# A hybrid trunk on one core: up products in passes of 512 and 256 columns, and other start distances between weights and activations

## The chip, the cores and the metric

The kernel runs on one core of a Trainium2 chip. The metric is device time in microseconds (us) of one launch, and less is better. The time before is the median of three runs; one more run was profiled, and its trace is what the sections below quote.

## What is computed

A two-layer trunk over 256 tokens of width 2048, in float32. Layer 0 is differential attention, layer 1 a gated DeltaNet (a chunked linear recurrence); each is followed by the same feed-forward, and each of the four parts is added to the residual `x`. The reference, cut to what matters here:

```python
D_MODEL, SEQ, DEPTH = 2048, 256, 2
D_FF = ((8 * D_MODEL // 3 + 127) // 128) * 128        # 5504 = 43 * 128

def conv_ffn(h, w_up, conv_w, conv_b, w_down):
    u = causal_dwconv(h @ w_up, conv_w) + conv_b       # w_up: 2048 x 11008
    val, gate = jnp.split(u, 2, axis=-1)
    return (jax.nn.silu(gate) * val) @ w_down          # w_down: 5504 x 2048

for i in range(DEPTH):
    h = rms_norm(x, mixer_norm[i])
    x = x + (diff_attention(h, ...) if i % 2 == 0 else gated_deltanet(h, ...))
    x = x + conv_ffn(rms_norm(x, ffn_norm[i]), ffn_w_up[i], ffn_conv_w[i], ffn_conv_b[i], ffn_w_down[i])
```

## The kernel before

Everything is held with the features on the 128 partitions and the 256 tokens along the free axis. A float32 product is made out of float32r matmuls, a shorter format: every weight chunk is cut into a rounded part `whi` (ScalarE, `nc.scalar.copy`, L89) and a remainder `wlo` (VectorE, L90), and every activation tile likewise holds a rounded half and a remainder half side by side, 2 x 256 columns. A product of one 128 x 128 weight tile with one activation tile is then three passes of 256 columns that add up in PSUM: `whi` with the rounded half (L116), `wlo` with the rounded half (L117), `whi` with the remainder half (L118). The text calls these three a **product**. Before each pass TensorE loads the 128 x 128 weights anew (rows PEld in the profile), while the pass before is still streaming.

`dense` makes one **block** of such products: an output of 256 features (two column tiles `c`) by 256 tokens, over `kt` row tiles, in chunks of four row tiles that arrive by one 512 KB DMA each. A block with `kt` = 16 is 32 products or 96 passes. In the order of time the blocks are: 16 for q and k of the attention (`w_qk`), then 4 blocks of `dense_tok` for v (`w_v`), 8 for `w_o`; in the feed-forward 43 up blocks (`w_up`, `kt` = 16, each holds one value tile and one gate tile) and 8 down blocks (`w_down`, `kt` = 43, 86 products each); in the DeltaNet 32 blocks of `w_in`, 8 of `dense_tok` for z and 32 of `w_out` (`kt` = 8) in four groups of heads, among small matmuls of the recurrence; then the second feed-forward. `dense_tok` has the roles turned: activations are the stationary 128 x 128 tile and 512 columns of weights stream past (L137 to L139).

The order of the instructions on an engine is the order in which the code is written, and nothing but semaphores on tiles holds an engine back. PSUM for the blocks is two tiles `ps` of two banks each, taken in turn.

**Distances.** The argument `dist` sets where in its buffer a weight chunk starts. Weight tiles have 128 words of room at their end, and the chunk is written `(place - x) % 128` words behind the tile's start, where `place` is the start of the activations modulo 128 words. So `x` is the distance in four-byte words, modulo 128, from the start of the weights that are being loaded to the start of the activations that stream meanwhile; one number for `whi`, one for `wlo`. Before, q and k, `w_in` and `w_out` take 13, 42, 45 and 12 in turn by head or by group of heads, `w_o`, the gate block, the up blocks of layer 1 from the second on and its down blocks take 51. In layer 0 the up blocks run through a list in which 13, 42 and 45 stand in turn between the values 0, 24, 37, 32, 17, 7 and 48 (so 0, 13, 0, 42, 0, 45, 24, 13, ...), and the down blocks take 13, 0, 13, 42, 0, 42, 45, 51. `dense_tok` has weights and activations at distance 0.

Of the kernel before, what the change touches and what calls it, by code (L numbers as in the profile page):

```python
# [11 lines left out]
ALU = mybir.AluOpType  # L12
# [4 lines left out]
P = 128  # L17
T = 256
# [1 line left out]
KD = D // P  # L20
EPS = 1e-6
CK = 4
BEST = 13, 42, 45
HP, AP, OP = 40, 48, 112
LNEXP = "natural_log_exp_and_others"

# [1 line left out]
class Trunk:  # L28
# [69 lines left out]
    def banks(self):  # L98
        return self.dps.tile([P, 2, 2 * T], F32, tag="ps", name="ps")

    def dense(self, w, kt, acts, place, tiles=2, lead=0, dist=(51, 51)):


        nc = self.nc
        ps = self.banks()
        for k0, nk in self.chunks(kt, CK, lead):
            hi, lo = self.weights(w[:, k0:k0 + nk, :], [(place - x) % P for x in dist])
            steps = [(k, c) for k in range(nk) for c in range(tiles)]
            if k0 + nk == kt:
                steps = [(k, c) for c in range(tiles) for k in range(nk)]  # L110
            for k, c in steps:
                a = acts(k0 + k)
                first, last = k0 + k == 0, k0 + k == kt - 1
                s = slice(c * P, (c + 1) * P)
                o = ps[:, c, :T]
                nc.tensor.matmul(o, hi[:, k, s], a[:, 0, :], start=first, stop=False)  # L116
                nc.tensor.matmul(o, lo[:, k, s], a[:, 0, :], start=False, stop=False)  # L117
                nc.tensor.matmul(o, hi[:, k, s], a[:, 1, :], start=False, stop=last)  # L118
            self.tick()
        return ps  # L120

    def merge(self, ps, u):

        self.nc.vector.tensor_tensor(u, ps[:, :, :T], self.rstd.unsqueeze(1).to_broadcast([P, 2, T]), ALU.mult)  # L124

    def dense_tok(self, w, kt, acts):

        nc = self.nc
        ps = self.banks()
        for k0, nk in self.chunks(kt, CK // 2):  # L130
            hi, lo = self.weights(w[:, k0:k0 + nk, :], (HP, HP))
            for k in range(nk):
                a = acts(k0 + k)
                first, last = k0 + k == 0, k0 + k == kt - 1
                for c in range(2):
                    ah, al = (a[:, i, c * P:(c + 1) * P] for i in range(2))
                    nc.tensor.matmul(ps[:, c, :], ah, hi[:, k, :], start=first, stop=False)  # L137
                    nc.tensor.matmul(ps[:, c, :], ah, lo[:, k, :], start=False, stop=False)  # L138
# [89 lines left out]
    def add_out(self, blk, ps, done):  # L228

        x = self.x[:, 2 * blk:2 * blk + 2, :]  # L230
        self.nc.vector.tensor_tensor(x, ps[:, :, :T], x, ALU.add)
        if done:
            for c in range(2):
                done(2 * blk + c)
            self.add_squares()

    def project(self, w, kt, acts, place, done, final=False, dists=[(51, 51)] * 8):

        n = KD // 2
        for b in range(n):  # L240
            ps = self.dense(w[b], kt, acts, place, dist=dists[b])
            if b < n - final:
                self.add_out(b, ps, done)
                continue
            for c in range(2):
                k = 2 * b + c
                self.nc.vector.tensor_tensor(self.x[:, k, :], ps[:, c, :T], self.x[:, k, :], ALU.add)
                done(k)

    def ffn(self, w_up, w_down, nj, cols_ap, done, final=False):  # L250

        nc = self.nc
        self.spawn(self.norm_stat())
        with self.tc.tile_pool(name="fp", bufs=1) as fp:
            cols = fp.tile([P, 8 * nj + 64], F32, tag="fcols", name="fcols")[:, :8 * nj]
# [3 lines left out]
            if final:  # L259
                ups, downs = [(12, 12)] + [(51, 51)] * (nj - 1), [(51, 51)] * 8  # L260
            else:
                ups = [(x, x) for y in (0, 24, 37, 32, 17, 7, 48) for z in BEST for x in (y, z)] + [(13, 13)]
                downs = [(x, x) for x in (13, 0, 13, 42, 0, 42, 45, 51)]
            rows = self.rows(fp.tile([P, nj * 2 * T + 8], F32R, tag="ac", name="ac"), nj, 0)
            for j in range(nj):
                ps = self.dense(w_up[j], KD, self.h_acts, HP, dist=ups[j])
                c = []
                u = fp.tile([P, 2, T], F32, tag="u", name="u", bufs=2)
                self.merge(ps, u)
# [12 lines left out]

    def attention(self, w_qk, w_v, w_o, nh, dist_ap, ident_ap, qg, kg, lvec, sub, start, done, lambda_init):

        nc, mp = self.nc, self.mp
        with self.tc.tile_pool(name="at", bufs=1) as at:
# [34 lines left out]
            def normed(ps, gain):  # L321
                r = at.tile([P, 2, T], F32, tag="qkr", name="qkr", bufs=3)
                self.merge(ps, r)
                sq = squares(r)
                qn = at.tile([P, 2, T], F32, tag="qkn", name="qkn", bufs=4)

                def go():
                    yield
                    pn = mp()
                    self.total(pn, [sq])  # L330
                    ri = at.tile([P, 2, T], F32, tag="ri", name="ri", bufs=2)
                    self.rsqrt(ri, pn, P)
# [60 lines left out]
            aTs = []  # L393
            for h in range(nh):
                acts, lead = (self.h_acts, 0) if h else (start, 1)
                mine = 2 * ((BEST + (12,))[h % 4],)
                qn, go = normed(self.dense(w_qk[h], KD, acts, HP, lead=lead, dist=mine), qgs)
                self.spawn(go)
                kn, go = normed(self.dense(w_qk[nh + h], KD, self.h_acts, HP, dist=mine), kg)
                aT = at.tile([P, 384], F32, tag=f"aT{h}", name="aT")  # L400
                self.spawn(weigh(h, qn, kn, go, aT))
                aTs.append(aT)
            for h in range(0, nh, 2):
                pv = self.dense_tok(w_v[h // 2], KD, self.h_acts)
# [12 lines left out]
    def gdn(self, w_gate, w_in, w_z, w_out, nb, hb, gate_ap, const_ap, hot_ap, conv_col, ng, done):  # L417
# [12 lines left out]
        with tc.tile_pool(name="gd", bufs=1) as gd:  # L430
# [235 lines left out]

            def out(b, acts):
                for blk in range(KD // 2):
                    ps = self.dense(w_out[b * (KD // 2) + blk], 2 * hb, lambda k: self.await_(acts, k), OP, dist=2 * ((BEST + (12,))[b % 4],))
# [4 lines left out]
            pend = None  # L674
            for b in range(nb):
                heads = range(b * hb, (b + 1) * hb)
                mine = 2 * ((BEST + (12,))[b % 4],)
# [5 lines left out]
                for op, i in plan + [("v", i) for i in range(1, hb)]:  # L683
                    if op == "k":
                        hq = heads[i]
                        c = convs(lin(self.dense(w_in[hq * 2], KD, self.h_acts, HP, dist=mine)), (hq, nq + hq))
                        self.spawn(keys(hq, c, cc, 2 * i, lqs))
                        if i == hb - 1:
                            self.spawn(invert(cc, lqs, inv))
                    elif op == "z":  # L690
                        gr = groups[i]
                        zt = zts[i] = gd.tile([P, 2, gv, P], F32, tag="vz", name="zt", bufs=4)
                        ps = self.dense_tok(w_z[heads[gr[0]] // 2], KD, self.h_acts)
                        for t in range(2):
                            nc.scalar.activation(zt[:, t].rearrange(flat), ps[:, t, :], AF.Silu,
                                                 scale=self.rstdc[:, t:t + 1])
                    else:
                        gi = i // gh
                        gr = groups[gi]
                        if i == gr[0]:  # L700
# [4 lines left out]
                        c = convs(lin(self.dense(w_in[hq * 2 + 1], KD, self.h_acts, HP, dist=mine)),  # L705
                                  (2 * nq + 2 * hq, 2 * nq + 2 * hq + 1))
                        self.spawn(to_tokens(c, vt, 2 * (i - gr[0]), ready))
                if pend:
# [204 lines left out]
```

## Time and profile before

| | us |
|---|---|
| time, median of 3 runs (lowest to highest) | 2715.84 (2714.43 to 2718.64) |
| the profiled run's own time | 2715.1 |
| its span, first to last instruction | 2713.3 |
| TensorE busy | 2699.1 |
| VectorE busy | 1852.9 |
| ScalarE busy | 1453.5 |

The span is what the trace covers, the time has 1.8 us more around it. The ends of matmuls are modelled in such a profile, and matmuls overlap: how fast TensorE goes is read from the distance between the starts of two matmuls, or from the length of a stretch and the number of matmuls in it, and not from its busy share.

### The profile page before, as it was taken

The page shows a single profiled execution, that of the slowest core. Times are in us where ns is not written, and L with a number is a line of the kernel's source. Part 1 is how long each engine was busy: PE and PEld are TensorE (multiplying, and loading weights), DVE is VectorE, ACT ScalarE, POOL GpSimd, SP SyncE. Part 2 cuts the span into 40 slices and gives each one's busy share as a digit, 9 for nine tenths or more (in the row PEclk, how much of TensorE's full clock was granted, in tenths as well). Part 3 has the DMA queues.
Part 4 walks back from the last instruction along what each step waited for, and adds up shares of the span by engine and source line. Part 5 has one row for each costly group of instructions (what it writes and reads, how often), then busy time and mean ns, then how long its engine had stood idle before and what let it go on. Part 6 is the DMA issues. An engine that isn't in the chain of part 4 may idle for free.

```text
span 2713.3 us, 53669 instructions
## 1 busy us (share of the span) xinstructions
PE 2699.1 (99%) x22352; PEld 2628.1 (97%) x22352; DVE 1852.9 (68%) x2719; ACT 1453.5 (54%) x1994; POOL 118.0 (4%) x220
## 2 busy tenths in 40 slices
PE   8999999999999999999999999999999999999999
PEld 8998999999999999999989989999999999999999
DVE  7776566666767554589688688679677777776444
ACT  6555555555555444484574574484465555554333
POOL 0000000000000000012021021021000000000000
PEclk9999999999999999999999999999999999999999
DMA  6555565666666666645355455455456666666665
GB/s 208 168 169 177 157 199 184 188 186 188 191 187 194 178 189 186 184 151 176 123 157 163 140 158 169 140 162 173 128 194 194 195 193 191 196 194 197 204 200 167
DMA packets 135396, 481.62 MB, mean 178 GB/s; under 512 B 15344, under 2 KB 18416, under 8 KB 135152
## 3 DMA queue, kind: packets, MB, share of 16 engines
q1 hardware_dynamic: 134000, 475.57, 57.7%
q8 instruction: 175, 2.87, 0.4%
q10 hardware_dynamic: 1152, 2.61, 0.3%
q14 instruction: 69, 0.57, 0.1%
HBM read 476.03 MB, written 2.10 MB: 176 GB/s over the span
## 4 chain that ended last, share of the span: by engine, by line
PE 99%; ACT 0%; DVE 0%; DMA 0%; issue 0%; ACTq 0%; SPq 0%; DVEq 0%
PE ps L117 27%; PE ps L116 27%; PE ps L118 27%; PE ps L137 3%; PE ps L138 3%; PE ps L139 3%; PE mp L615 2%; PE mp L225 1%; PE mp L503 1%; PE mp L558 0%; PE mp L567 0%; PE mp L480 0%; PE mp L585 0%; PE mp L579 0%; PE mp L594 0%; PE mp L502 0%
## 5 line engine op out<-in xcount | busy, mean ns | idle before, releaser
L90 DVE TENSOR_TENSOR wlo<-raw,whi 128x1024 fp32r<-128x1024 f32 (+2 forms) x909 | 1110.0, 1222 | 670.0 <-ACT whi L89 666.6
L89 ACT CAST whi<-raw 128x1024 fp32r<-128x1024 f32 (+2 forms) x909 | 948.4, 1044 | 1055.0 <-PE ps L118 871.1
L116 PE MATMUL ps<-h,whi 128*128 128x256 f32 x4304 | 1201.2, 279 | 7.5 <-ACT h L151 5.9
L117 PE MATMUL ps<-h,wlo 128*128 128x256 f32 x4304 | 1202.1, 279 | 2.7 <-DVE wlo L90 2.7
L118 PE MATMUL ps<-h,whi 128*128 128x256 f32 x4304 | 1200.5, 279 | 0.0
L116 PEld LDWEIGHTS ps<-h,whi 128*128 128x128 f32 x4304 | 810.6, 188 | 10.3 <-ACT h L151 5.9
L117 PEld LDWEIGHTS ps<-h,wlo 128*128 128x128 f32 x4304 | 811.8, 189 | 6.5 <-DVE wlo L90 3.4
L118 PEld LDWEIGHTS ps<-h,whi 128*128 128x128 f32 x4304 | 811.8, 189 | 1.3
L116 PE MATMUL ps<-ac,whi 128*128 128x256 f32 x1632 | 453.7, 278 | 0.0
L117 PE MATMUL ps<-ac,wlo 128*128 128x256 f32 x1632 | 453.6, 278 | 0.0
L118 PE MATMUL ps<-ac,whi 128*128 128x256 f32 x1632 | 453.5, 278 | 0.0
L117 PEld LDWEIGHTS ps<-ac,wlo 128*128 128x128 f32 x1632 | 307.5, 188 | 0.0
L116 PEld LDWEIGHTS ps<-ac,whi 128*128 128x128 f32 x1632 | 307.5, 188 | 0.0
L118 PEld LDWEIGHTS ps<-ac,whi 128*128 128x128 f32 x1632 | 307.4, 188 | 0.0
L137 PE MATMUL ps<-whi,h 128*128 128x512 f32 x384 | 150.7, 393 | 0.0
L138 PE MATMUL ps<-wlo,h 128*128 128x512 f32 x384 | 150.0, 391 | 0.0
L139 PE MATMUL ps<-whi,h 128*128 128x512 f32 x384 | 149.9, 390 | 0.0
L116 PE MATMUL ps<-oc,whi 128*128 128x256 f32 x512 | 144.3, 282 | 0.0
L117 PE MATMUL ps<-oc,wlo 128*128 128x256 f32 x512 | 143.7, 281 | 0.0
L118 PE MATMUL ps<-oc,whi 128*128 128x256 f32 x512 | 143.7, 281 | 0.0
L206 DVE SCALAR_TENSOR_TENSOR cv<-u,fcols,cv 128x255 f32<-128x255 f32 (+1 forms) x344 | 142.9, 478 | 0.0
L124 DVE TENSOR_TENSOR u<-ps,rstd 128x512 f32<-128x512 f32 x118 | 81.4, 690 | 45.8 <-PE ps L118 45.5
(201 smaller groups left out, 2221.8 us busy)
## 6 DMA issues: line engine op xcount, KB each, us to landing
raw<-w_up SPq DMA_DIRECT2D x344, 512.0 KB, 4.3
raw<-w_down SPq DMA_DIRECT2D x160, 512.0 KB, 4.0
raw<-w_in SPq DMA_DIRECT2D x128, 512.0 KB, 4.1
raw<-w_z SPq DMA_DIRECT2D x64, 512.0 KB, 3.8
raw<-w_out SPq DMA_DIRECT2D x64, 512.0 KB, 3.7
raw<-w_qk SPq DMA_DIRECT2D x63, 512.0 KB, 4.2
raw<-w_v SPq DMA_DIRECT2D x32, 512.0 KB, 3.7
raw<-w_o SPq DMA_DIRECT2D x32, 512.0 KB, 4.4
```

What stands on the lines that cost most here:

```text
L89: nc.scalar.copy(hi, raw)
L90: nc.vector.tensor_tensor(lo, raw, hi.bitcast(F32), ALU.subtract)
L116: nc.tensor.matmul(o, hi[:, k, s], a[:, 0, :], start=first, stop=False)
L117: nc.tensor.matmul(o, lo[:, k, s], a[:, 0, :], start=False, stop=False)
L118: nc.tensor.matmul(o, hi[:, k, s], a[:, 1, :], start=False, stop=last)
L124: self.nc.vector.tensor_tensor(u, ps[:, :, :T], self.rstd.unsqueeze(1).to_broadcast([P, 2, T]), ALU.mult)
L137: nc.tensor.matmul(ps[:, c, :], ah, hi[:, k, :], start=first, stop=False)
L138: nc.tensor.matmul(ps[:, c, :], ah, lo[:, k, :], start=False, stop=False)
L139: nc.tensor.matmul(ps[:, c, :], al, hi[:, k, :], start=False, stop=last)
L206: nc.vector.scalar_tensor_tensor(out[:, j:], u[:, :T - j], taps[n - 1 - j], out[:, j:], ALU.mult, ALU.add)
L225: last = self.nc.tensor.matmul(out, self.onesr, p[:, j], start=i + j == 0, stop=i + j == n)
L615: nc.tensor.matmul(p[:, v, :], l(v), r[:, v, :], start=i == 0, stop=i == len(terms) - 1)
```

## The change

The up products of both feed-forwards are made of two passes: `whi` with both halves of the activations at once (512 columns, into both halves of a PSUM bank), and `wlo` with the rounded half (256 columns, added to the first half of the bank). `merge` then brings the two halves together: ScalarE copies the second half out of PSUM, VectorE adds the first half, and VectorE multiplies by the norm's factor, where one VectorE multiplication did before. Each of the 86 up blocks has a distance of its own, 0 to 42 in layer 0, 43 to 63 and then 3, 6, ... to 66 in layer 1, the same for `whi` and `wlo`. The down blocks of layer 0 are made in pairs of passes too, at eight pairs of distances (the first number is for `whi`), and `add_out` adds both halves into `x`, one after the other. All other `dense` blocks stand at 45 words, which is 180 bytes. The weights of `dense_tok` go through 48 distances of the list `TOK`, one for every two chunks of two row tiles.

```diff
-BEST = 13, 42, 45
+TOK = [x for x in range(64) if x % 4 or x > 32 and x not in (32, 48)]
...
-    def dense(self, w, kt, acts, place, tiles=2, lead=0, dist=(51, 51)):
+    def dense(self, w, kt, acts, place, tiles=2, lead=0, dist=(45, 45), pair=False):
...
                 o = ps[:, c, :T]
+                if pair:
+                    nc.tensor.matmul(ps[:, c, :], hi[:, k, s], a, start=first, stop=False)
+                    nc.tensor.matmul(o, lo[:, k, s], a[:, 0, :], start=False, stop=last)
+                    continue
                 nc.tensor.matmul(o, hi[:, k, s], a[:, 0, :], start=first, stop=False)
                 nc.tensor.matmul(o, lo[:, k, s], a[:, 0, :], start=False, stop=False)
                 nc.tensor.matmul(o, hi[:, k, s], a[:, 1, :], start=False, stop=last)
...
-    def merge(self, ps, u):
+    def merge(self, ps, u, pair=False):
+        if pair:
+            self.nc.scalar.copy(u, ps[:, :, T:])
+            self.nc.vector.tensor_tensor(u, ps[:, :, :T], u, ALU.add)
+            self.nc.vector.tensor_tensor(u, u, self.rstd.unsqueeze(1).to_broadcast([P, 2, T]), ALU.mult)
+            return
         self.nc.vector.tensor_tensor(u, ps[:, :, :T], self.rstd.unsqueeze(1).to_broadcast([P, 2, T]), ALU.mult)
...
-        for k0, nk in self.chunks(kt, CK // 2):
-            hi, lo = self.weights(w[:, k0:k0 + nk, :], (HP, HP))
+        for i, (k0, nk) in enumerate(self.chunks(kt, CK // 2)):
+            hi, lo = self.weights(w[:, k0:k0 + nk, :], 2 * ((HP + dists[i // 2]) % P,))
...
-        self.nc.vector.tensor_tensor(x, ps[:, :, :T], x, ALU.add)
+        for i in range(1 + pair):
+            self.nc.vector.tensor_tensor(x, ps[:, :, i * T:(i + 1) * T], x, ALU.add)
...
-                ps = self.dense(w_up[j], KD, self.h_acts, HP, dist=ups[j])
+                ps = self.dense(w_up[j], KD, self.h_acts, HP, dist=2 * ((j if not final else 43 + j if j < 21 else 3 * j - 60),), pair=True)
...
-            self.project(w_down, nj, lambda k: acts[k], AP, done, final, downs)
+            self.project(w_down, nj, lambda k: acts[k], AP, done, final, None if final else [(53, 8), (58, 8), (53, 40), (58, 40), (12, 8), (53, 60), (58, 60), (53, 52)])
...
-                qn, go = normed(self.dense(w_qk[h], KD, acts, HP, lead=lead, dist=mine), qgs)
+                qn, go = normed(self.dense(w_qk[h], KD, acts, HP, lead=lead), qgs)
```

On TensorE, in the middle of the up blocks of layer 0, a chunk before is a row of passes like these (`h` are the activations, the last number is the output's columns):

```order
5001 L116 MATMUL ps_7505<-h_75,whi_7597 128x256
5002 L117 MATMUL ps_7505<-h_75,wlo_7598 128x256
5003 L118 MATMUL ps_7505<-h_75,whi_7597 128x256
5004 L116 MATMUL ps_7505<-h_75,whi_7597 128x256
5005 L117 MATMUL ps_7505<-h_75,wlo_7598 128x256
5006 L118 MATMUL ps_7505<-h_75,whi_7597 128x256
```

The same place in the changed kernel:

```order
3208 L119 MATMUL ps_5165<-h_75,whi_5189 128x512
3209 L120 MATMUL ps_5165<-h_75,wlo_5190 128x256
3210 L119 MATMUL ps_5165<-h_75,whi_5189 128x512
3211 L120 MATMUL ps_5165<-h_75,wlo_5190 128x256
3212 L119 MATMUL ps_5165<-h_75,whi_5189 128x512
```

Two passes stand where three stood, with two loads of weights instead of three, and the columns that stream in a product are 768 in both.

On VectorE, one up block before, from the merge on (`u` is the merged block, `cv` the convolution, `ac` the split output):

```order
437 L124 TENSOR_TENSOR u<-ps,rstd 128x512
438 L90 TENSOR_TENSOR wlo<-raw,whi 128x1024
439 L206 SCALAR_TENSOR_TENSOR cv<-u,fcols,cv 128x255 x2
440 L206 SCALAR_TENSOR_TENSOR cv<-u,fcols,cv 128x254 x2
441 L90 TENSOR_TENSOR wlo<-raw,whi 128x1024
442 L277 TENSOR_TENSOR cv<-cv 128x256
443 L90 TENSOR_TENSOR wlo<-raw,whi 128x1024
444 L218 TENSOR_TENSOR ac<-cv,ac 128x256
445 L90 TENSOR_TENSOR wlo<-raw,whi 128x1024
```

The same block in the changed kernel:

```order
461 L132 TENSOR_TENSOR u<-ps,u 128x512
462 L133 TENSOR_TENSOR u<-u,rstd 128x512
463 L90 TENSOR_TENSOR wlo<-raw,whi 128x1024
464 L217 SCALAR_TENSOR_TENSOR cv<-u,fcols,cv 128x255 x2
465 L217 SCALAR_TENSOR_TENSOR cv<-u,fcols,cv 128x254 x2
466 L90 TENSOR_TENSOR wlo<-raw,whi 128x1024
467 L284 TENSOR_TENSOR cv<-cv 128x256
468 L90 TENSOR_TENSOR wlo<-raw,whi 128x1024
469 L229 TENSOR_TENSOR ac<-cv,ac 128x256
470 L90 TENSOR_TENSOR wlo<-raw,whi 128x1024
```

The merge is two VectorE instructions ahead of the next remainder `wlo`, and the first of them waits for ScalarE's copy.

## Rows read from the trace of the kernel before

**Rows 1.** The page: engines' busy time and share; TensorE's granted clock in 40 slices.

```profile
PE 2699.1 (99%) x22352; PEld 2628.1 (97%) x22352; DVE 1852.9 (68%) x2719; ACT 1453.5 (54%) x1994; POOL 118.0 (4%) x220
...
PEclk9999999999999999999999999999999999999999
```

**Rows 2.** The page: the chain that ended last, by engine.

```profile
PE 99%; ACT 0%; DVE 0%; DMA 0%; issue 0%; ACTq 0%; SPq 0%; DVEq 0%
```

**Rows 3.** TensorE's waits: who for whom, us in total, times, longest.

```profile
PE ps L116 <- ACT h L151: 5.9, 1, 5.9
PE ps L117 <- DVE wlo L90: 2.7, 3, 1.4
```

**Rows 4.** Windows, matmuls into `ps`: window, length, busy (x count), clock, DMA, GB/s.

```profile
402.00:884.80 482.80, 482.17 (x4131) 1.00 0.62 189
884.80:1128.20 243.40, 243.40 (x2067) 1.00 0.62 182
2006.30:2475.40 469.10, 468.69 (x4131) 1.00 0.64 194
```

**Rows 5.** The same view, windows of single blocks and of 100 us.

```profile
426.20:437.72 11.52, 11.52 (x99) 1.00 0.58 183
437.70:448.90 11.20, 11.20 (x99) 1.00 0.60 187
460.40:471.30 10.90, 10.90 (x98) 1.00 0.61 189
471.30:482.81 11.51, 11.51 (x98) 1.00 0.59 188
819.50:830.40 10.90, 10.90 (x99) 1.00 0.64 194
1149.40:1160.90 11.50, 11.50 (x98) 1.00 0.60 181
1652.30:1663.20 10.90, 10.90 (x99) 1.00 0.63 186
1961.50:1983.90 22.40, 22.40 (x195) 1.00 0.60 203
2100.00:2200.00 100.00, 100.00 (x885) 1.00 0.65 193
```

**Rows 6.** Timeline of TensorE in `dense_tok`: start, length, engine, line, instruction.

```profile
1231.97 0.39 PE L137 MATMUL ps<-whi,h 128*128 128x512 f32 x1
...
1232.65 0.39 PE L137 MATMUL ps<-whi,h 128*128 128x512 f32 x1
```

**Rows 7.** The same view around a matmul of the DeltaNet between two of `dense_tok`.

```profile
1596.36 0.40 PE L137 MATMUL ps<-whi,h 128*128 128x512 f32 x1
1596.60 0.40 PE L225 MATMUL mp<-qp,onesr 128*128 128x512 f32 x1
1596.83 0.39 PE L138 MATMUL ps<-wlo,h 128*128 128x512 f32 x1
...
1597.53 0.39 PE L138 MATMUL ps<-wlo,h 128*128 128x512 f32 x1
```

**Rows 8.** Groups by line and shape: count, busy us, mean ns, idle before and releaser.

```profile
L124 DVE TENSOR_TENSOR u<-ps,rstd 128x512 f32<-128x512 f32 x118 | 81.4, 690 | 45.8 <-PE ps L118 45.5
L231 DVE TENSOR_TENSOR x<-ps,x 128x512 f32<-128x512 f32 x55 | 37.8, 688 | 25.4 <-PE ps L118 25.2
L595 ACT COPY vt<-mp 128x512 f32<-128x512 f32 x16 | 9.4, 588 | 28.9 <-PE mp L594 28.6
```

**Rows 9.** Windows, all engines, one up block: PE, PEld, DVE, ACT, POOL busy.

```profile
2029.30:2040.20 10.90, 10.90 (x99) 10.90 (x98) 7.76 (x11) 5.92 (x8) 0.00 (x0) 1.00 0.62 194
```

More of the change, by code (lines that the diff above doesn't have):

```diff
@@ L120, in dense, with dense_tok @@
         return ps
-    def merge(self, ps, u):
+    def merge(self, ps, u, pair=False):
[4 more added lines that the diff above has]
+            return
         self.nc.vector.tensor_tensor(u, ps[:, :, :T], self.rstd.unsqueeze(1).to_broadcast([P, 2, T]), ALU.mult)
-    def dense_tok(self, w, kt, acts):
+    def dense_tok(self, w, kt, acts, dists):
         nc = self.nc
         ps = self.banks()
-        for k0, nk in self.chunks(kt, CK // 2):
-            hi, lo = self.weights(w[:, k0:k0 + nk, :], (HP, HP))
+        for i, (k0, nk) in enumerate(self.chunks(kt, CK // 2)):
+            hi, lo = self.weights(w[:, k0:k0 + nk, :], 2 * ((HP + dists[i // 2]) % P,))
             for k in range(nk):
@@ L226, in total, with add_out @@
         return last
-    def add_out(self, blk, ps, done):
+    def add_out(self, blk, ps, done, pair=False):
         x = self.x[:, 2 * blk:2 * blk + 2, :]
-        self.nc.vector.tensor_tensor(x, ps[:, :, :T], x, ALU.add)
+        for i in range(1 + pair):
+            self.nc.vector.tensor_tensor(x, ps[:, :, i * T:(i + 1) * T], x, ALU.add)
         if done:
@@ L235, in add_out, with project @@
             self.add_squares()
-    def project(self, w, kt, acts, place, done, final=False, dists=[(51, 51)] * 8):
+    def project(self, w, kt, acts, place, done, final=False, pairs=None):
         n = KD // 2
         for b in range(n):
-            ps = self.dense(w[b], kt, acts, place, dist=dists[b])
+            ps = self.dense(w[b], kt, acts, place, dist=pairs[b] if pairs else (45, 45), pair=bool(pairs))
             if b < n - final:
-                self.add_out(b, ps, done)
+                self.add_out(b, ps, done, bool(pairs))
                 continue
@@ L258, in ffn @@
             acts = []
[L259 to L263, printed above, removed]
             rows = self.rows(fp.tile([P, nj * 2 * T + 8], F32R, tag="ac", name="ac"), nj, 0)
             for j in range(nj):
-                ps = self.dense(w_up[j], KD, self.h_acts, HP, dist=ups[j])
+                ps = self.dense(w_up[j], KD, self.h_acts, HP, dist=2 * ((j if not final else 43 + j if j < 21 else 3 * j - 60),), pair=True)
                 c = []
                 u = fp.tile([P, 2, T], F32, tag="u", name="u", bufs=2)
-                self.merge(ps, u)
+                self.merge(ps, u, True)
                 for half in range(2):
@@ L395, in attention @@
                 acts, lead = (self.h_acts, 0) if h else (start, 1)
-                mine = 2 * ((BEST + (12,))[h % 4],)
-                qn, go = normed(self.dense(w_qk[h], KD, acts, HP, lead=lead, dist=mine), qgs)
+                qn, go = normed(self.dense(w_qk[h], KD, acts, HP, lead=lead), qgs)
                 self.spawn(go)
-                kn, go = normed(self.dense(w_qk[nh + h], KD, self.h_acts, HP, dist=mine), kg)
+                kn, go = normed(self.dense(w_qk[nh + h], KD, self.h_acts, HP), kg)
                 aT = at.tile([P, 384], F32, tag=f"aT{h}", name="aT")
@@ L403, in attention @@
             for h in range(0, nh, 2):
-                pv = self.dense_tok(w_v[h // 2], KD, self.h_acts)
+                pv = self.dense_tok(w_v[h // 2], KD, self.h_acts, TOK[2 * h:2 * h + 4])
                 v = at.tile([P, 2, 2 * T], F32, tag="v", name="v", bufs=2)
@@ L668, in out @@
                 for blk in range(KD // 2):
-                    ps = self.dense(w_out[b * (KD // 2) + blk], 2 * hb, lambda k: self.await_(acts, k), OP, dist=2 * ((BEST + (12,))[b % 4],))
+                    ps = self.dense(w_out[b * (KD // 2) + blk], 2 * hb, lambda k: self.await_(acts, k), OP)
                     self.add_out(blk, ps, done if b == nb - 1 else None)
@@ L676, in gdn @@
                 heads = range(b * hb, (b + 1) * hb)
-                mine = 2 * ((BEST + (12,))[b % 4],)
                 cc = gd.tile([P, 32, 32], F32, tag="s4", name="Cc", bufs=3)
@@ L685, in gdn @@
                         hq = heads[i]
-                        c = convs(lin(self.dense(w_in[hq * 2], KD, self.h_acts, HP, dist=mine)), (hq, nq + hq))
+                        c = convs(lin(self.dense(w_in[hq * 2], KD, self.h_acts, HP)), (hq, nq + hq))
                         self.spawn(keys(hq, c, cc, 2 * i, lqs))
@@ L692, in gdn @@
                         zt = zts[i] = gd.tile([P, 2, gv, P], F32, tag="vz", name="zt", bufs=4)
-                        ps = self.dense_tok(w_z[heads[gr[0]] // 2], KD, self.h_acts)
+                        ps = self.dense_tok(w_z[heads[gr[0]] // 2], KD, self.h_acts, TOK[16 + 8 * b + 4 * i:20 + 8 * b + 4 * i])
                         for t in range(2):
@@ L704, in gdn @@
                         hq = heads[i]
-                        c = convs(lin(self.dense(w_in[hq * 2 + 1], KD, self.h_acts, HP, dist=mine)),
+                        c = convs(lin(self.dense(w_in[hq * 2 + 1], KD, self.h_acts, HP)),
                                   (2 * nq + 2 * hq, 2 * nq + 2 * hq + 1))
```

## The prediction

> **What bounds the kernel now.** [...] The chain that ended last is TensorE for 99% [rows 2], and its longest waits for data are 5.9 us once and 2.7 in three pieces [rows 3]. So nothing on another engine is worth anything here; the time is the number of passes times the interval between their starts. What the reader is to see in the windows is that this interval is not one number. A block of 96 passes takes 10.90 us at 51, 45 and 48 (100 us hold 882 passes, 113.3 ns each), but 11.52 us at distance 0 (120.0 ns), 11.51 at 24, 11.50 at 13 in the DeltaNet and 11.20 us at 42 behind a block at 0; at 12, four blocks of 48 passes take 22.40 us, 116.7 ns [rows 5]. The work is the same; only the place of the weights differs. And there is memory in it: 13 also runs at 10.90 us, in the block that begins at 819.50 us, behind one at 48 [rows 5]. 45 was quick even behind a block at 0 (the window from 460.40) [rows 5].
>
> **The steps.** The base is the profiled run, 2715.1 us (span 2713.3 and 1.8 around it), 0.7 below the median of 2715.84.
>
> *Up blocks, -3 us.* Both stages take 482.8 + 469.1 us now, of which 1.0 us is idle at their edges [rows 4], for 86 x 32 = 2752 products: 345.5 ns each on average, 340.0 at the quick 51. A pass of 512 columns is in the trace: in `dense_tok`, three of them take 0.68 us, 226.7 ns each, at distance 0 [rows 6]. That is twice 113.3 ns, so a product of two passes has a floor of 226.7 + 113.3 = 340.0 ns, no less than the three passes have at a quick distance. What can be won is only the price of a bad distance, paid twice instead of three times, and perhaps not at all in the long pass, where the load of the next weights has 113 ns to spare. For the short pass I take the mean of the bad rows, 6.7 (0), 6.6 (24), 6.5 (13) and 3.3 (12): 5.8 ns. For the long pass the rows give 0 (it runs at 226.7 at distance 0, where the short one loses 6.7) and, behind a foreign matmul, 0.70 us for three, 6.7 ns more each [rows 7]. Distance 0 is the nearer row, being a steady stream; I take 1 ns, and keep 0 and 6.7. Which of the 86 distances are bad? Of those seen, 42 and above are quick, below that all but 13 slow at every place; I set the border at 40. Between 52 and 63 there is no row, and I take these as quick. Then 40 blocks of layer 0 are bad, and in layer 1 the thirteen from 3 to 39 and 66 (as 2, if it repeats after 64): 54 at 346.8 ns, 32 at 340.0. Mean 344.3, 1.2 less than now, times 2752: -3 us. Layer 0 gets quicker and layer 1, which stands at the floor now, gets slower.
>
> *45 instead of 13, 42 and 12, -14 us.* q and k, `w_in` and `w_out` have 1536 passes at each of the four (384 + 768 + 384). Against 45 at 113.3 ns (the window from 1652.30), 13 at 120.0 loses 10.3 us, 12 at 116.7 loses 5.1, 42 between 0 and 3.3 ns, say 1, loses 1.5 [rows 5]: 17 us. A sixth off, since 13 is quick at times, and since matmuls of the recurrence come between many of these passes: 14. Bounds 6 (only 12's part and a little of 42's) and 17. 51 to 45 in `w_o` and the second down stage costs nothing: both stand at 10.90 [rows 5].
>
> [...]
>
> *Down blocks of layer 0, -8 us.* 243.4 us for 688 products are 353.8 ns now [rows 4], since five of the eight stand at 0, 13 or a 42 behind them. The new `whi` distance is 53 or 58 in seven blocks, which I took as quick, the `wlo` one 8, 40, 60 or 52, which matters under the long pass; 342 ns gives 235.3 us. Bounds 229 (see the first rival) and 243 (353.4 ns, both passes 6.7 late).
>
> *`dense_tok`, +1 us.* 1152 passes leave distance 0, where they run at the floor. 31 of the 48 new distances lie below 40; 1 ns on these is 0.7 us. Bounds 0 and +5 (6.7 ns).
>
> *Merge and add, +1 us.* Each up block gets a PSUM copy on ScalarE (588 ns by L595) and one more VectorE instruction of some 690 ns, each down block of layer 0 another 688 [rows 8]. In a block of 10.90 us VectorE is busy 7.76 and ScalarE 5.92 [rows 9], so both fit under TensorE. `wlo` of a coming chunk stands behind the merge on VectorE, and would be some 0.6 + 0.7 us later there; with three buffers of four row tiles, and a chunk 2.7 us long, TensorE does not reach it. Without this cover it would be 86 x 1.3 = 112 us. Only behind the last down block of layer 0 does the extra add lie bare, 0.7 us, since the DeltaNet waits for it.
>
> Sum: -3 - 14 - 8 + 1 + 1 = -23, and 2715.1 - 23 = **2692 us**. With the long pass at 0 to 3 ns, 45 at -10 to -17 and the down blocks at -5 to -10, this case reaches from 2685 to 2706.
>
> **Rivals.** *A pass has a fixed part (2673 us).* Distance 0 costs a short pass 6.7 ns. If the long pass at distance 0 holds the same 6.7, its true floor is 220.0 ns, and a product falls to 333.3 at quick distances and 344.9 at bad ones, 340.6 over the 86: 4.9 x 2752 = -13 us; the down blocks come to some 335 ns, -13; `dense_tok` gains 3 at its quick distances; with -14 and +1 that is -42. For it: 120.0 - 113.3 and the equal step between both lengths. Against it: no pass of 512 columns that I saw is under 226.7 [rows 6, 7]. [...] No row here shows a fixed part: 226.7 is just twice 113.3.
>
> *The gains stay small (2712 to 2719 us).* With 4 ns more on every product than I took, some 349, the up blocks lose 10 us, the down blocks gain 3, `dense_tok` loses 3, and where matmuls of the recurrence come between, 45 settles no better than the others: -6. Together +4 with the merge. For it: 42 and 13 show that the interval hangs on what went before. Against: 45 recovered behind 0.
>
> *The two lengths never fall into step (2729 us, slower).* In steady streams all passes are of one length. If 512 and 256 in turn keep every pass 6.7 ns late, as the three behind a foreign matmul [rows 7], a product takes 353.4 ns at all distances: up +22, down 0, `dense_tok` at 31 bad distances +5, 45 still -14, merge +1: +14. The point from which it decides: a mean over the 3440 products above 352 ns. Against it: behind the disturbance `dense_tok` comes back to 226.7.
>
> **How the numbers follow.** The likeliest case gets 0.57, the fixed part 0.22, small gains 0.12, out of step 0.09. A difference of 0.2%, 5.4 us, is about what a measurement of this kernel can tell from none. Faster by that is nearly all of the first two and a part of the third: 0.80; the same 0.11; slower 0.09. The range goes from below the fixed-part case to the upper end of the likeliest case and the lower one of the third: 2668 to 2712. It leaves out the slow case and most of the third, under 2 in 10.
>
> **What would show it.** In the profile after, up blocks of the second half of layer 1 in steps of 32 products: 10.9 us at quick distances and 11.1 at bad ones, layer 0 near 11.1 throughout. A block under 10.8 us speaks for the fixed part, blocks over 11.2 for the lengths out of step. The window from 884.8 should shrink to 235 us, and blocks of `w_in` and `w_out` free of other matmuls to 113.3 ns a pass. Wrong would make it a region of quick distances that ends at 51, which costs 32 x 6.8 ns in each of some 20 blocks, 4 us, or waits for `wlo` among TensorE's waits.

## The result, and the profile after

The changed kernel takes 2720.6 us (median of 18 runs, 2718.3 to 2723.0) where the kernel before takes 2715.7 on the same chip: a ratio of 1.0019, 95% interval 1.0012 to 1.0026. It is 5 us slower, just inside the 0.2% that the prediction called no difference, but 29 us above the 2692 that was forecast and above the whole of its range, 2668 to 2712. The profiled run's span is 2716.8 us, 3.5 more than before.

The page says what it said before [rows 1, 2]: TensorE is busy 99% of the span at a granted clock of 0.9 or more in every slice, and it is the chain that ended last. The idle time in the last column stands at 0.0 for both new lines, and neither is among TensorE's waits, so no pass of an up block waits for data.

```profile
PE 2701.9 (99%) x18912; PEld 2474.2 (91%) x18912; DVE 1909.1 (70%) x2813; ACT 1489.6 (55%) x2077; POOL 120.1 (4%) x220
...
PEclk9999999999999999999999999999999999999999
...
PE 99%; DMA 0%; ACT 0%; DVE 0%; issue 0%; SPq 0%; DVEq 0%; ACTq 0%
...
L119 PE MATMUL ps<-h,whi 128*128 128x512 f32 x2752 | 964.9, 394 | 0.0
L120 PE MATMUL ps<-h,wlo 128*128 128x256 f32 x2752 | 772.8, 281 | 0.0
```

The windows of the stages (columns as in rows 4) show where the time went: the up blocks of layer 0, its down blocks, the up blocks of layer 1, and the DeltaNet between.

```profile
401.60:883.90 482.30, 481.67 (x2755) 1.00 0.62 189
883.90:1125.70 241.80, 241.80 (x1379) 1.00 0.63 183
1994.70:2478.90 484.20, 483.57 (x2755) 1.00 0.62 188
1125.70:1994.70 869.00, 740.39 (x5426) 1.00 0.52 158
```

Against [rows 4]: layer 0's up blocks 0.5 us less, its down blocks 1.6 less, layer 1's up blocks 15.1 more; the DeltaNet's stretch was 878.1 between the same two windows, so 9.1 less, and everything ahead of the first up block is 0.4 less. Together +3.5, the whole difference of the spans. Some 3 of the 9.1 are not the change's, by estimate (3.4 us twice at half the clock lose 3.4): in the trace before, TensorE's granted clock falls to 0.50 for 3.4 us twice in this stretch, and passes of 256 columns start 213 ns apart there, against 113.3 to 120.0 in the blocks of [rows 5]; in the trace after it does not fall in this stretch. The windows before, all matmuls:

```profile
1143.30:1146.70 3.40, 3.40 (x18) 0.50 0.72 231
1300.30:1303.70 3.40, 3.40 (x18) 0.50 0.06 25
```

Windows of single blocks of the same kernel: the up blocks at 45, 49 and 52 words, and one block of `w_in` at 45.

```profile
2017.10:2028.40 11.30, 11.30 (x67) 1.00 0.63 184
2062.40:2074.00 11.60, 11.60 (x65) 1.00 0.62 190
2096.60:2107.70 11.10, 11.10 (x66) 1.00 0.65 185
1149.50:1160.40 10.90, 10.90 (x98) 1.00 0.65 190
```

In three passes 45 words give 10.90 us, here in `w_in` as in [rows 5]; in two passes the same 45 words give 11.30. From the starts of the matmuls the 86 up blocks take 11.08 to 11.62 us each (the first of a stage without the interruption that lies in it), and none the 10.88 (340.0 ns a product) on which the forecast counted for 32 of them. The mean is 11.22 us, 350.6 ns a product; between neighbouring products the timeline of TensorE shows it (at 45, start and modelled length): three products in 1.06 us, 353 ns each.

```profile
2019.89 0.39 PE L119 MATMUL ps<-h,whi 128*128 128x512 f32 x1
2020.13 0.28 PE L120 MATMUL ps<-h,wlo 128*128 128x256 f32 x1
...
2020.95 0.39 PE L119 MATMUL ps<-h,whi 128*128 128x512 f32 x1
```

### The profile page after: what moved, and what is told of

It is laid out like the page before. It is cut to its first block, busy times and chain, and to the rows that moved or that the text cites. A ratio compares the mean times of both kernels' runs of the same rounds, so it can differ in the third digit from the quotient of the medians.

```text
span 2716.8 us, 46973 instructions
## 1 busy us (share of the span) xinstructions
PE 2701.9 (99%) x18912; PEld 2474.2 (91%) x18912; DVE 1909.1 (70%) x2813; ACT 1489.6 (55%) x2077; POOL 120.1 (4%) x220
## 4 chain that ended last, share of the span: by engine, by line
PE 99%; DMA 0%; ACT 0%; DVE 0%; issue 0%; SPq 0%; DVEq 0%; ACTq 0%
PE ps L119 29%; PE ps L120 15%; PE ps L123 13%; PE ps L122 12%; PE ps L124 12%; PE ps L149 3%; PE ps L150 3%; PE ps L148 3%; PE mp L621 2%; PE mp L236 1%; PE mp L509 1%; PE mp L564 0%; PE mp L573 0%; PE mp L486 0%; PE mp L585 0%; PE mp L591 0%
## 5 line engine op out<-in xcount | busy, mean ns | idle before, releaser
L119 PE MATMUL ps<-h,whi 128*128 128x512 f32 x2752 | 964.9, 394 | 0.0
L119 PEld LDWEIGHTS ps<-h,whi 128*128 128x128 f32 x2752 | 516.8, 188 | 120.6
L122 PE MATMUL ps<-h,whi 128*128 128x256 f32 x1552 | 433.1, 280 | 7.9 <-ACT h L162 5.9
L124 PE MATMUL ps<-h,whi 128*128 128x256 f32 x1552 | 432.3, 279 | 0.0
L122 PEld LDWEIGHTS ps<-h,whi 128*128 128x128 f32 x1552 | 292.4, 189 | 10.3 <-ACT h L162 5.9
L124 PEld LDWEIGHTS ps<-h,whi 128*128 128x128 f32 x1552 | 293.1, 189 | 1.1
L122 PE MATMUL ps<-ac,whi 128*128 128x256 f32 x944 | 260.5, 276 | 0.0
L124 PE MATMUL ps<-ac,whi 128*128 128x256 f32 x944 | 260.3, 276 | 0.0
L119 PE MATMUL ps<-ac,whi 128*128 128x512 f32 x688 | 241.8, 395 | 0.0
L122 PEld LDWEIGHTS ps<-ac,whi 128*128 128x128 f32 x944 | 177.1, 188 | 0.1
L123 PEld LDWEIGHTS ps<-ac,wlo 128*128 128x128 f32 x944 | 177.1, 188 | 0.0
L124 PEld LDWEIGHTS ps<-ac,whi 128*128 128x128 f32 x944 | 177.1, 188 | 0.0
L119 PEld LDWEIGHTS ps<-ac,whi 128*128 128x128 f32 x688 | 129.5, 188 | 30.8
L148 PE MATMUL ps<-whi,h 128*128 128x512 f32 x384 | 152.8, 398 | 0.0
```

The costliest lines, as they stand in the source:

```text
L119: nc.tensor.matmul(ps[:, c, :], hi[:, k, s], a, start=first, stop=False)
```

## The experiments

Three theories stood at the start. **Out of step**: a change of length between passes costs time, 64 of them in an up block. **The long pass**: a pass of 512 columns is late at any distance but 0. **Slow distances**: the new distances are slow ones, also in three passes. Each time is the median of its runs; before measured 2713.9 to 2716.4 beside them. "Floor" is 340.0 ns a product, 10.88 us for an up block.

**Three passes and 45 words everywhere** (`x1_all45`, against before; `dense_tok` stays at 0).

```diff
-    def dense(self, w, kt, acts, place, tiles=2, lead=0, dist=(51, 51)):
+    def dense(self, w, kt, acts, place, tiles=2, lead=0, dist=(45, 45), pair=False):
...
-                ps = self.dense(w_up[j], KD, self.h_acts, HP, dist=ups[j])
+                ps = self.dense(w_up[j], KD, self.h_acts, HP, dist=(45, 45))
...
-            self.project(w_down, nj, lambda k: acts[k], AP, done, final, downs)
+            self.project(w_down, nj, lambda k: acts[k], AP, done, final)
```

> All blocks in three passes of 256 columns, as before the change, and all at 45 words; dense_tok at distance 0. Nothing of the computation is left out, here and in all kernels that follow. If the loss of the changed kernel lies in the pairs of 512 and 256 columns (out of step, or the 512-column pass late at other distances than 0), every block is at the floor: up blocks 10.88 us in both layers (up stages 469 and 469 us), down blocks 29.24, w_in 10.88, and the time is 2715.7 - 13.8 (up, layer 0) - 9.5 (down, layer 0) - 12 (q, k, w_in, w_out) = 2680 us, 2677 to 2685. If 45 is quick only in the second layer or only in short stretches, the up blocks of layer 0 stay at 11.2 us and the time is 2692 or more.

Measured: 2679.0 us, ratio 0.9868 (0.9851 to 0.9884). Its stage windows, in the order layer 0 up, down, DeltaNet, layer 1 up:

```profile
399.30:868.00 468.70, 468.07 (x4130) 1.00 0.64 194
868.00:1102.00 234.00, 234.00 (x2067) 1.00 0.65 190
1102.00:1967.30 865.30, 738.23 (x5427) 1.00 0.51 159
1967.30:2436.00 468.70, 468.29 (x4130) 1.00 0.64 194
```

Both feed-forwards stand at the floor. What the changed kernel lost lies in its pairs of passes, its distances or both, and not in 45 words.

**`dense_tok` back at distance 0** (`x2_tok0`, against the changed kernel).

```diff
-            hi, lo = self.weights(w[:, k0:k0 + nk, :], 2 * ((HP + dists[i // 2]) % P,))
+            hi, lo = self.weights(w[:, k0:k0 + nk, :], (HP, HP))
```

> The changed kernel with dense_tok alone back at distance 0. Its twelve blocks took 22.2 to 23.3 us in the changed kernel and 21.8 to 22.4 before. If a 512-column pass is slower at other distances than 0, the blocks come back to 21.8 to 22.4 and the time falls by 4 to 7 us from the changed kernel's 2720.6, to 2714 to 2717. If the blocks are slow because of what runs between them, the time stays at 2719 to 2722.

Measured: 2715.6 us, ratio to before 1.0004 (0.9995 to 1.0013); 5 us less than the changed kernel, 4 when each is set against the runs of before beside it, as expected of a 512-column pass that is late at other distances. From the starts, the twelve blocks took 264.4 us before, 271.5 in the changed kernel and 265.3 here.

**Passes of one length together** (`x3_grouped45`: up blocks at 45, in each chunk eight passes of 512 columns, then eight of 256; all else as in `x1_all45`).

```diff
+            if pair:
+                for half in range(2):
+                    for k, c in steps:
...
+                        if half:
+                            nc.tensor.matmul(ps[:, c, :T], lo[:, k, s], a[:, 0, :], start=False, stop=last)
+                        else:
+                            nc.tensor.matmul(ps[:, c, :], hi[:, k, s], a, start=first, stop=False)
+                steps = []
```

> The up blocks in passes of 512 and 256 columns at 45 words, but in each chunk all eight 512-column passes first, then all eight 256-column passes; all other blocks in three passes at 45, dense_tok at 0. Same passes as the changed kernel's, 8 changes of length a block in place of 64. Theory 'out of step' (a change of length costs; 64 changes cost 0.34 us a block, 5.3 ns each): 10.92 us a block, time 2683 us (2679 to 2688). Theory 'the long pass is late at any distance but 0' (230 to 235 ns): 11.0 to 11.15 us a block, time 2690 to 2704. Theory 'the distances themselves are slow' (45 is not one): 10.88 us, 2681.

Measured: 2708.3 us, ratio 0.9976 (0.9967 to 0.9985), 11.20 us a block. The timeline of TensorE has one row for each run of eight:

```profile
469.90 2.02 PE L121 MATMUL ps<-h,whi 128*128 128x512 f32 x8
471.76 1.10 PE L119 MATMUL ps<-h,wlo 128*128 128x256 f32 x8
472.70 0.62 PE L121 MATMUL ps<-h,whi 128*128 128x512 f32 x2
```

Eight long passes take 1.86 us, 232.5 ns each, eight short ones 0.94, 117.5 each, with one change of length in eight passes. Grouping gives back 0.10 of the 0.42 us above the floor. "Out of step" is not the main cause.

**The changed kernel's distances in three passes** (`x6_three_sweep`: `x1_all45` with these in the up blocks).

```diff
+                ps = self.dense(w_up[j], KD, self.h_acts, HP, dist=2 * ((j if not final else 43 + j if j < 21 else 3 * j - 60),))
```

> Three passes in the up blocks, at the distances that the changed kernel gives them: 0 to 42 in layer 0, 43 to 63 and 3, 6, ... 66 in layer 1; the rest at 45 in three passes, dense_tok at 0. Theories 'out of step' and 'the long pass is late at any distance but 0': the distances part into bad ones at 11.1 to 11.5 us and quick ones at 10.88, 45, 48 and 51 among the quick, and these blocks take other times than in the changed kernel, where none is under 11.08. By the prediction's assumption (40 and above quick, below bad) the up stages are 492 and 477 us and the time 2712. Theory 'the distances themselves are slow': each block takes in three passes what it takes in pairs, 11.08 to 11.62 us, the stages 482 and 484.

Measured: 2717.7 us (one run). Windows: both up stages, then the blocks at 13 (behind one at 12), 45, 48 (behind 47), 51, and 48 once more, behind 45.

```profile
399.80:890.00 490.20, 489.57 (x4131) 1.00 0.60 186
1990.60:2477.90 487.30, 486.89 (x4130) 1.00 0.60 187
548.90:559.80 10.90, 10.90 (x99) 1.00 0.63 193
2014.40:2025.30 10.90, 10.90 (x99) 1.00 0.61 191
2048.00:2059.30 11.30, 11.30 (x98) 1.00 0.59 189
2082.10:2093.00 10.90, 10.90 (x98) 1.00 0.62 193
2399.50:2410.40 10.90, 10.90 (x98) 1.00 0.64 196
```

Only 13, 42, 45, 51 and, behind 45, 48 are at the floor; the other 78 blocks take 11.1 to 11.8 us. So the border at 40 was wrong already in three passes: 43, 44, 46, 47, 49, 50 and 52 to 63 are all slow. "Slow distances" holds for most of them, but not as the whole cause: 13, 42, 45 and 51 are quick here and 11.1 to 11.3 us in pairs. The two stages are longer than in pairs (482.3 and 484.2): at the 78 slow distances a block in pairs is 0.18 us quicker on average.

**Two distances for the two passes** (`x4_pair_grid`; down blocks in three passes at 45, `dense_tok` at 0).

```diff
+                ps = self.dense(w_up[j], KD, self.h_acts, HP, dist=((45, (3 * j) % 64) if not final else ((3 * j) % 64, 45)), pair=True)
```

> The up blocks in alternating passes of 512 and 256 columns as in the changed kernel, but with different distances for the two: in layer 0 whi at 45 and wlo at 0, 3, 6, ... modulo 64, in layer 1 whi at 0, 3, 6, ... modulo 64 and wlo at 45; the down blocks in three passes at 45, dense_tok at 0. If each pass has quick distances of its own (the prediction's picture), some of the 86 blocks reach the floor, 10.88 us, and 45 under one of the two makes its pass quick in a whole stage. If a 512-column pass of these products is late at whatever distance, none is under 11.05 us, the stages are 480 to 485 us each, and the time is near 2706, as it was for the grouped passes.

Measured: 2712.0 us (one run). Windows of blocks of layer 0, `whi` at 45 and `wlo` at 54, 57, 60, then at 3 and at 45:

```profile
605.10:616.50 11.40, 11.40 (x67) 1.00 0.62 187
616.50:627.40 10.90, 10.90 (x66) 1.00 0.64 189
627.40:638.30 10.90, 10.90 (x67) 1.00 0.64 191
413.90:424.80 10.90, 10.90 (x67) 1.00 0.59 183
571.20:582.50 11.30, 11.30 (x66) 1.00 0.63 188
```

Three pairs of passes reach the floor, (45, 57), (45, 60) and (45, 3). The weights of the long pass stand at 45 in all five rows; it runs at 226 to 227 ns in the three quick ones and at 233.3 in (45, 45). While it streams, the weights of the short pass are loaded (in the trace after, which has the same order of passes, their load starts 3 ns behind the long pass, median of 2752), so it might hang on the `wlo` distance alone. It does not: in layer 1, with `wlo` at 45 throughout, it takes 229 to 238 ns by its starts, and in layer 0, with `whi` at 45 throughout, the short pass takes 113 to 122. "The long pass" falls as a theory, and so does the prediction's own picture of a price for each pass by its own distance. A fourth theory took their place, **fit**: a product of two passes is at the floor where the two distances fit together. That is a name for what was seen, and does not say why.

**`dense_tok`, one distance for each block** (`x5_tok_block`; all else as in `x1_all45`).

```diff
+            hi, lo = self.weights(w[:, k0:k0 + nk, :], 2 * ((HP + dists) % P,))
...
+                pv = self.dense_tok(w_v[h // 2], KD, self.h_acts, (8, 20, 32, 45)[h // 2])
...
+                        ps = self.dense_tok(w_z[heads[gr[0]] // 2], KD, self.h_acts, (3, 48, 13, 51, 26, 58, 38, 53)[2 * b + i])
```

> Three passes at 45 everywhere, and each of the twelve blocks of dense_tok (passes of 512 columns alone) at one distance: 8, 20, 32, 45 for v and 3, 48, 13, 51, 26, 58, 38, 53 for z. At 0 they take 21.76 us where nothing runs between and up to 22.4 else. Theory 'out of step' (only a change of length costs): the quick distances 45, 48 and 51 give 226.7 ns a pass, as 0 does. Theory 'the long pass is late at any distance but 0': all blocks at 230 to 236 ns, 22.2 us and more, and the time 4 to 8 us above the kernel at 45 with dense_tok at 0 (2679).

Measured: 2687.3 us (one run), 8 above `x1_all45`. Windows of the blocks at 48 and 53, and then of the same two blocks in `x1_all45`, at 0:

```profile
1205.10:1227.50 22.40, 22.40 (x97) 1.00 0.62 190
1809.10:1832.00 22.90, 22.90 (x97) 1.00 0.63 198
```

```profile
1200.90:1222.70 21.80, 21.80 (x98) 1.00 0.64 196
1798.70:1820.50 21.80, 21.80 (x98) 1.00 0.66 209
```

No change of length stands in these blocks, and yet they lose 0.6 and 1.1 us. 45, the quick distance of three passes, is among the slowest here, 22.86 us by its starts against 21.92 at 0. Which distances are quick hangs here on the pattern of passes and not on the distance alone.

**Grouped passes at all 86 distances** (`x7_grouped_sweep`: `x3_grouped45` with the changed kernel's distances in the up blocks).

> The grouped kernel (in each chunk eight passes of 512 columns, then eight of 256), with the changed kernel's 86 distances in the up blocks in place of 45. At 45 the grouped block took 11.20 us and the alternating one 11.30. Theory 'out of step': every distance gains what the change of length costs, 0.1 us or more, and those that are quick for both lengths reach 10.9. Theory 'the long pass is late at any distance but 0': 512-column passes in their runs of eight at 226.7 ns at distance 0 alone, 230 to 236 elsewhere, blocks between 11.05 and 11.5, mean as in the changed kernel within 0.05 us (11.22).

Measured: 2713.0 us (one run); the mean block is 11.22 us, that of the changed kernel. The lowest is 57, 10.99 us, whose timeline is:

```profile
2150.61 1.98 PE L121 MATMUL ps<-h,whi 128*128 128x512 f32 x8
2152.43 1.10 PE L119 MATMUL ps<-h,wlo 128*128 128x256 f32 x8
2153.36 1.98 PE L121 MATMUL ps<-h,whi 128*128 128x512 f32 x8
```

Eight long passes in 1.82 us, with the change of length within it: the long pass is at its floor at 57, far from 0, where the short one is not (0.93 us for eight). At 0 the long passes run at 231 ns by their starts. That ends "the long pass" in its own ground, and "out of step" too, since 64 changes of length or 8 give the same mean.

**45 words in q and k, `w_in` and `w_out` alone** (`x8_only45`, against before).

```diff
-                mine = 2 * ((BEST + (12,))[h % 4],)
+                mine = (45, 45)
```

> The kernel before with one part of the change alone: q and k, w_in and w_out at 45 words in place of 13, 42, 45 and 12 in turn. The prediction put this at -14 us (6 to 17): 2701 us. From the kernel with 45 everywhere, where the stretch between the feed-forwards lasted about 12 us less than before: -13, 2702 us. If 45 is quick there only because the feed-forward ahead of it is changed too: 2708 or more.

Measured: 2701.9 us, ratio 0.9948 (0.9930 to 0.9966): -14 us, interval 9 to 19. The span is 11.9 shorter; windows from the first block to the last of layer 0's up stage, and of the DeltaNet:

```profile
399.90:882.70 482.80, 482.17 (x4131) 1.00 0.61 189
...
1126.10:1994.50 868.40, 741.41 (x5427) 1.00 0.51 158
```

2.1 us ahead of the first and 9.7 in the second. The same DeltaNet takes 865.3 in `x1_all45`. The 3.1 us between the two are the clock's, by the same estimate: in this trace it stands at 0.50 for 3.4 us from 1292.8 and again from 1890.1 us, as it does twice in the trace before, and in the trace of `x1_all45` nowhere in the stretch.

**Pairs that fit** (`x9_pair_fit`: the up blocks of `x4_pair_grid` at these distances).

```diff
+                ps = self.dense(w_up[j], KD, self.h_acts, HP, dist=((45, 3) if not final else (45, 60)), pair=True)
```

> Up blocks in alternating passes of 512 and 256 columns, whi at 45 throughout, wlo at 3 in layer 0 and at 60 in layer 1 (the two that reached 10.88 us in the sweep); down blocks in three passes at 45, dense_tok at 0: the kernel with 45 everywhere, with the up blocks in pairs. Theory 'a product is at the floor where the two distances fit together': 10.88 us in all 86 blocks, stages of 469 us, time 2679 us as with three passes at 45, 2677 to 2684 with the longer merge, and nothing to be won over it, since 226.7 + 113.3 is 340.0. Theory 'the floor was reached only in the wake of the neighbouring blocks': blocks of 11.1 to 11.3 us again, 2700 to 2712.

Measured: 2690.0 us, ratio 0.9910 (0.9894 to 0.9927), between the two cases. Windows of the two up stages:

```profile
400.30:869.10 468.80, 468.17 (x2754) 1.00 0.63 194
1968.40:2446.30 477.90, 477.27 (x2754) 1.00 0.63 190
```

At (45, 3) all blocks behind the first run at 10.88 us, with 64 changes of length in each. At (45, 60) they run at 11.09: in `x4_pair_grid` that pair was quick only in the wake of (45, 57). Half of the expectation missed, and the miss is the memory that [rows 5] show for 13.

**Is it the difference of the two?** (`x10_pair_diff`.)

```diff
+                ps = self.dense(w_up[j], KD, self.h_acts, HP, dist=((3 * j) % 64, ((3 * j) % 64 + (15 if final else 22)) % 64), pair=True)
```

> The up blocks in alternating passes, whi at 0, 3, 6, ... modulo 64 in both layers, wlo 22 further in layer 0 (as 45 and 3 modulo 64) and 15 further in layer 1 (as 45 and 60). Theory 'the difference of the two distances decides': most of the 86 blocks at 10.88 us, stages near 470, time 2680 to 2688. Theory 'each place counts by itself, the difference tells nothing': only the blocks at (45, 3) and (45, 60) and a few others at the floor, the mean at 11.15 to 11.25 us, time 2706 to 2713.

Measured: 2708.1 us (one run). Windows: both stages, with the blocks at (42, 0) and (45, 3) of the first.

```profile
400.00:882.00 482.00, 481.37 (x2754) 1.00 0.64 189
557.60:568.50 10.90, 10.90 (x67) 1.00 0.67 188
568.50:579.40 10.90, 10.90 (x67) 1.00 0.63 192
1986.10:2468.20 482.10, 481.47 (x2754) 1.00 0.63 189
```

Two of 86 blocks are at the floor. The difference does not decide; (42, 0) is one more pair that fits, reached from a slow neighbour.

**The changed kernel with its up blocks at (45, 3)** (`x11_after_fit`, one line against the changed kernel).

```diff
-                ps = self.dense(w_up[j], KD, self.h_acts, HP, dist=2 * ((j if not final else 43 + j if j < 21 else 3 * j - 60),), pair=True)
+                ps = self.dense(w_up[j], KD, self.h_acts, HP, dist=(45, 3), pair=True)
```

> The changed kernel with one thing replaced: all 86 up blocks at (45, 3) in place of their 86 distances; pairs of passes, the down blocks' pairs, dense_tok's distances and 45 elsewhere as in the changed kernel. If the time above the prediction lies in the up blocks' distances alone, their stages fall from 482.3 and 484.2 to 469 each, 28.5 us: 2692 us (2689 to 2696). If the pairs have another price that the blocks' starts do not show, it stays above 2700; if the second layer's blocks drift from the floor as they did at (45, 60): 2701.

Measured: 2689.5 us, ratio 0.9912 (0.9899 to 0.9926): 31 us less than the changed kernel from the one line, 29.1 by the two traces' spans, and 28.9 of these lie in the two up stages. Their windows:

```profile
402.60:871.40 468.80, 468.17 (x2755) 1.00 0.63 194
...
1980.90:2449.70 468.80, 468.17 (x2754) 1.00 0.63 194
```

**Pairs at (45, 3) wherever the change has pairs** (`x12_all_fit`: `x9_pair_fit` with (45, 3) in both layers and in the down blocks of layer 0).

```diff
+            self.project(w_down, nj, lambda k: acts[k], AP, done, final, None if final else [(45, 3)] * 8)
```

> Pairs of passes at (45, 3) in all up blocks and in the down blocks of layer 0, three passes at 45 elsewhere, dense_tok at 0. If (45, 3) fits for any pair of passes, up stages of 469 us, down blocks of 29.24 us, and 2679 us (2677 to 2683), the time of three passes at 45: the pair then has neither a gain nor a price. If it fits only the activations of the up products: the down blocks at 29.8 to 30.9 us as in the changed kernel, 2684 to 2692.

Measured: 2678.3 us, ratio 0.9871 (0.9858 to 0.9885), the time of `x1_all45`. Windows (up, down, up) and the timeline of TensorE in an up block:

```profile
401.60:870.40 468.80, 468.17 (x2754) 1.00 0.63 194
870.40:1104.40 234.00, 234.00 (x1379) 1.00 0.65 189
1970.40:2439.20 468.80, 468.17 (x2754) 1.00 0.63 194
```

```profile
799.70 0.39 PE L119 MATMUL ps<-h,whi 128*128 128x512 f32 x1
799.92 0.28 PE L120 MATMUL ps<-h,wlo 128*128 128x256 f32 x1
...
800.72 0.39 PE L119 MATMUL ps<-h,whi 128*128 128x512 f32 x1
```

Three products in 1.02 us, 340 ns each: pairs of passes reach the floor, for other activations (`ac`) too, and have no price beyond it. Nor have they a gain: 2678.3 and 2679.0 us cannot be told apart. Both beat the kernel before by 36 us.

## Why the prediction was wrong

| term | forecast, us | measured, us | from |
|---|---|---|---|
| up blocks | -3 | +14.6 | stage windows |
| 45 words | -14 | -14 (9 to 19) | `x8_only45` |
| down blocks of layer 0 | -8 | -1.6 | stage window |
| `dense_tok` | +1 | +4 to +7 | `x2_tok0`; twelve blocks by their starts |
| merge and add | +1 | none seen | `x12_all_fit` beside `x1_all45` |

*The step that failed is the up blocks' price per product*, 344.3 ns forecast and 350.6 measured, 17.6 us over both stages. It carried three assumptions. The border at 40, drawn from four quick distances and no row between them: in three passes only 13, 42, 45, 48 and 51 are quick, and three of these not always (48 in `x6_three_sweep`, 13 and 42 in [rows 5]). A region that ends at 51 was among the prediction's own signs of being wrong, at 4 us; what came were single values. That a distance which is quick in three passes is quick in two: none of them was, and both 45 and 51 give 11.30 us. And 1 ns for the long pass at a bad distance, from its steady stream at distance 0 [rows 6], where the row behind a foreign matmul [rows 7] had 6.7: with `whi` and `wlo` at one distance the long pass came to 226 to 240 ns by its starts. Behind the first block of each stage it took 232.3 ns on average, 5.6 above its floor, and the short pass 118.3, 5.0 above; over all blocks the forecast had 0.6 and 3.6. So 5.0 of the 6.3 ns by which the product was mis-sized are the long pass. Replacing the 86 distances by (45, 3) alone moved the kernel to 2689.5, within the forecast's own range of 2685 to 2706.

*The down blocks* failed by the same step: 53 and 58 as quick distances for `whi`. They took 351.5 ns a product where 342 were forecast; (45, 3) gives 340.

*`dense_tok`* was mis-sized: 1 ns on 31 distances was forecast, while 45 and 48, quick by the border at 40, lose 0.6 to 0.9 us a block too (`x5_tok_block`). Its bound of +5 was about right.

*45 words* was right in kind and size, and *the merge* was hidden as argued: TensorE's waits for `wlo` stayed at 2.0 us in all, 2.7 before [rows 3].

*The rivals.* By time "the gains stay small" came nearest, 2712 to 2719 us with some 349 ns a product where 350.6 came; but it had 45 words at -6. Its reason, that the interval hangs on what went before, has a part, as (45, 60) shows, yet in the changed kernel no block reached the floor behind any neighbour. "The two lengths never fall into step" gave 2729 us, with 353.4 ns at all distances; the mean over the 3440 products is 350.8, under the 352 from which it was to decide. Its sign was right and its reason was not: two lengths in turn run at the floor at (45, 3), 340 ns a product, and passes of one length run above it at other distances, 22.86 us for a block of `dense_tok` at 45 against 21.92 at 0. "A pass has a fixed part" is refuted: its floor of 333.3 ns is 10.67 us a block, and in all 14 traces no up block is under 10.88. And the place of the weights alone moves the time: the same passes in the same order take 482.3 us in layer 0's up stage of the changed kernel and 468.8 in `x11_after_fit`.

What stays open is why two distances fit. The runs moved the weights alone; that the distance counts and not the weights' address is borne out, not shown, by 45 in three passes, at the floor for activations that the code places at 40, 48 and 112 words, and by (45, 3) in pairs for two of these. Equal distances did not fit in any of the 86 blocks of the changed kernel, the difference of the two does not tell, and what went before has a part in it, (45, 60) at 10.88 behind (45, 57) and 11.09 behind itself. The traces show starts of passes, not what a load or a stream waits for.

## What to carry to other kernels

Where TensorE is at its bound in such a stream of small passes, measure each pattern of passes with its place in memory as one thing: a distance that was quick for one pattern was not so for the next (45 gave 10.88 us a block in three passes, 11.30 in two), and most values between quick ones were slow (78 of 86 blocks, in three passes). Fewer passes with the same columns win nothing by themselves here, for at the floor a long pass takes 226.7 ns, twice the 113.3 of the short one. One value that has been seen to recover the floor from a slow neighbour, and is then used throughout, was worth 36 us; the changed kernel, which spreads its blocks over many, is some 41 behind it.

## What was unexpected

The interval has levels: in the pairs most blocks lie at 340.0, 346.7, 350.0 or 353.3 ns a product (10.88, 11.09, 11.20, 11.30 us), and a block keeps its level to 0.01 us through a whole stage, as at (45, 60).

There seem to be two kinds of quick distance, some of them seen once or twice only. 45 in three passes, (45, 3), (45, 57) and (42, 0) in pairs come to the floor from a slow block; 48 in three passes and (45, 60) in pairs keep it if the block before had it and run at 11.31 and 11.09 us otherwise. 13 in three passes is of neither kind: in layer 0 before, it comes to the floor behind 24 (the window from 482.8) and not behind 37 (11.52 us from 550.0).

At a slow distance a pair of passes is mostly quicker than three: 11.22 against 11.40 us on average over the 78 of `x6_three_sweep`, quicker by more than 0.01 us at 65 of them. A comparison at one such distance shows a gain that the quick one does not have.
